# A hybrid attention, state-space and convolution layer: 24 modulation tiles moved from two projection loops into the attention heads

## Chip, cores and metric

One Trainium2 chip, one core. The metric is the time of one execution on the device in microseconds (us), lower is better. In the rows PE is TensorE (matmuls), PEld its weight loads, DVE is VectorE, ACT is ScalarE, POOL is GpSimd and SP is the engine that only starts transfers. Each engine runs its instructions in the order in which they stand in its queue; an instruction that waits holds up everything behind it on that engine.

## What is computed

One layer of a diffusion backbone in float32, for 128 context tokens (with the vector `c_ctx`) and 512 latent tokens (with the vector `c`). Cut to what matters:

```python
mod = silu(c_vec) @ w_ada + b_ada                  # 6 x 1024 numbers for each vector
sh1, sc1, g1, sh2, sc2, g2 = split(mod, 6)
h = rmsnorm(x) * (1 + sc1) + sh1
cq, ckv, kr, z, xs, Bm, Cm, dt, gm, gs = split(h @ w_in)
q = rmsnorm(cq) @ w_uq; k, v = mla_kv(rmsnorm(ckv), kr, w_ukv)   # 8 heads, rotary on latents
p = softmax(q @ k.T * scale); o_mla = (p @ v) @ w_o_mla
xbc = silu(dwconv(xs, Bm, Cm)); y = chunked scan, both directions
o_ssd = rmsnorm(y * silu(z)) @ w_o_ssd
merged = sigmoid(gm) * o_mla + sigmoid(gs) * o_ssd
x = x + g1 * (merged @ w_out)
h2 = rmsnorm(x) * (1 + sc2) + sh2
u = dwconv(h2 @ w_up); x = x + g2 * ((silu(u1) * u2) @ w_down)
```

The change concerns the rows of `mod` that make `g1`, `sh2` and `sc2`: three times 1024 numbers, which is 24 tiles of 128 numbers, each for two vectors. They are first read in the output projection `w_out` (`g1`) and after it (`sh2`, `sc2`).

## The kernel before

All 640 tokens lie along the free axis and the features on the 128 partitions. A large product is made of three matmuls on rounded halves of both operands (`mm3`, L139): high by high, low by high, high by low. Each weight tile is loaded raw (`wload`, L129, the pool `ws` with four buffers of the tag `raw`), rounded by ACT (L115, `whi`) and its remainder made by POOL, or for some small tiles by DVE (L112, `wlo`). The order of PE is written out by hand.

**A modulation tile.** 16 modulation tiles are made on PE at the start. The other 32 are row products on DVE (`ada_rows`, L242 to L263): tile j has one load of 512 KB, a 128x1024 block of `w_ada` turned so that the outputs lie on the partitions (`araw`); two SCALAR_TENSOR_TENSOR of 128x1024 multiply it with the two conditioning vectors, laid on all partitions (`crow`, after a SiLU), and sum along the row into two columns of `mod` (L260); one TENSOR_SCALAR adds the bias to both columns (L261). Tiles 16 to 23 are gate 1, 24 to 31 shift 2, 32 to 39 scale 2 and 40 to 47 gate 2. Each call of `ada_next` makes one tile, with its instructions put behind that of the eviction given to it. The first eight stand in the loop over the eight row blocks of `w_o_mla` (after L837), eight in the loop over `w_o_ssd` (after L1093) and eight in the loop over `w_out` (after L1103); gate 2 is made later and is not touched.

**A head of the attention.** Eight heads run one behind the other, some 32.6 us each. The scores part has four blocks of 128 latent queries against 640 keys and one block of 128 context queries (`pc`). A block t puts its scores into two PSUM tiles of 128x320 (tag `sm`, four banks in a ring), then DVE takes the two row maxima (L591, TENSOR_REDUCE) and scales them (L592), ACT takes the exponentials out of both PSUM tiles (L594), DVE adds the two row sums (L598), inverts (L599) and normalises the block `p` (L600). So a bank is free for a later product when the exponential has read it, and the exponential waits for L592. With the ring of four, block 2 takes the banks of block 0, block 3 those of block 1, `pc` the first of block 2; then the query product of the next head, `lowrank` (L139 with `cqh`), takes the second bank of block 2 and the first of block 3. In an odd head the rotary queries of the next pair of heads come ahead of it (`rope_queries`): their weight is 256 wide and its remainder `wlo` is made by DVE. After the scores the values part turns the probabilities around (`flip`, L607, with the rounding on ACT and the remainder `ptl` on DVE, L112) and multiplies them with the values (L616). Between these products `fill` puts matmuls of other projections (`w_xbc`, `w_gm`), whose convolution (L465, L468, two instructions of 127 and two of 511 columns) or eviction runs on DVE and ACT. F_S, F_P, F_R, F_Q, F_K, F_T and F_V say how many fill products stand where; they do not change.

**The loops after.** In the `w_o_ssd` loop DVE evicts the PSUM tile `big` of each row block (L1092), adds the attention's share (L1093), and makes the remainder for `w_out` (L112); the next row block but one needs the bank that L1092 reads.

Of the kernel before, what the change touches and what calls it, by code (L numbers as in the profile page):

```python
# [10 lines left out]
F32 = mybir.dt.float32  # L11
# [46 lines left out]
D1, D2 = 2, 4  # L58
G0, G_T, G_C, G_S, G_Z, G_B, G_Y = 15, 1, 1, 1, (2, 2, 3, 2, 4), 3, 0
RP = 2  # L60


CHUNKS = (0, 8, 16)
# [16 lines left out]
def trunk_kernel(ctx: ExitStack, tc: tile.TileContext, a: dict):  # L80
# [15 lines left out]
    def page(dt=F32, pool=None):  # L96
        return (pool or pg).tile([128, T], dt, tag="pgr", name=nm("pg"))
# [141 lines left out]
        DVE.tensor_reduce(st[:m, 0:n, :], pt[:m].rearrange("p (i g r) -> p i r g", g=4, r=32)[:, :, 0:2, :], AX.X, ALU.add)  # L239
        return st  # L240

    def ada_rows(tiles, tile, nraw):  # L242


        crow = []
        for r in range(2):
            t = tile("crow", 2)
            nc.sync.dma_start(t, a["crow"][r : r + 1, :].to_broadcast([128, D]))
            ACT.activation(t, t, AF.Silu)
            crow.append(t)  # L250
        left = list(tiles)

        def step(after):
            j = left.pop(0)
            raw = tile("araw", nraw)
            nc.sync.dma_start(raw, a["w_adar"][j - 16])
            with tc.issue_after(after.ins):
                for r in range(2):
                    out = raw if r else tile("junk", 1)
                    DVE.scalar_tensor_tensor(out, raw, 1.0, crow[r], ALU.mult, ALU.mult, accum_out=mod[:, j, r : r + 1])  # L260
                DVE.tensor_scalar(mod[:, j, :], mod[:, j, :], vec[:, V_BADA + j : V_BADA + j + 1], None, ALU.add)  # L261

        return step  # L263
# [230 lines left out]
    def fill(n):  # L494
        for _ in range(n):
            next(streams[0], None)
# [1 line left out]

    att = ExitStack()
    ost = ExitStack()  # L500
    op = ost.enter_context(tc.tile_pool(name="op", bufs=8, side="right", reuse_waits="tile"))
    awk = ExitStack()
    ap = awk.enter_context(tc.tile_pool(name="ap", bufs=1, reuse_waits="tile"))

    cos = ap.tile([128, NS], F32)
    nc.scalar.dma_start(cos, a["rope"][0])
# [67 lines left out]
    def scores(q, qr, k, c0, ks, p):  # L574

        n = ks.stop - ks.start
        qc = slice(c0, c0 + 128)
        w = min(n, 320)
        parts = []
        for n0 in range(0, n, w):  # L580
            ps = small()
            parts.append((ps[:, 0:w], slice(ks.start + n0, ks.start + n0 + w)))
        mm3(parts, q[0][:, qc], q[1][:, qc], k, True, False)

        for k_ in krs:
            for sv, sl in parts:
                PE.matmul(sv, qr[:, qc], k_[:, sl], start=False, stop=k_ is krs[1])  # L587
        st = ap.tile([128, 8], F32, tag="st", name=nm("st"), bufs=6)
        n = len(parts)
        for i, (sv, _) in enumerate(parts):  # L590
            DVE.reduce_max(st[:, i : i + 1], sv, AX.X)  # L591
        DVE.tensor_scalar(st[:, 2:3], st[:, 0:1], st[:, n - 1 : n], -SCALE, ALU.max, ALU.mult)  # L592
        for i, (sv, _) in enumerate(parts):
            ACT.activation(  # L594
                p[:, i * w : (i + 1) * w], sv, AF.Exp, bias=st[:, 2:3], scale=SCALE, accum_out=st[:, 4 + i : 5 + i]
            )
        if n == 2:
            DVE.tensor_tensor(st[:, 4:5], st[:, 4:5], st[:, 5:6], ALU.add)  # L598
        DVE.reciprocal(st[:, 3:4], st[:, 4:5])  # L599
        DVE.tensor_scalar(p, p, st[:, 3:4], None, ALU.mult)  # L600

    def flip(probs, kt):

# [70 lines left out]
    with tc.manual_schedule(engines={PE.engine}):  # L674
# [8 lines left out]
        for h in range(H):  # L683
            hh = h % 2
            probs = []
            for t in range(4):
                p = ap.tile([128, 640], F32, tag="p", name=nm("p"), bufs=4)
                scores(q, qrs[hh], k, NP + 128 * t, keys, p)
                probs.append(p)
                fill(F_S[t])  # L690
            pc = ap.tile([128, 128], F32, tag="pc", name=nm("pc"))
            scores(q, qrs[hh], k, 0, ctx_keys, pc)
# [8 lines left out]
                q = next(qk)  # L701
                fill(F_Q)
            fill(F_K if nxt else F_K + 2)
            o = page(F32, op)
            oT.append(o)
            pts = []
            for kt in range(LAG):
# [5 lines left out]
            for kt in range(5):  # L713
# [4 lines left out]
                if kt + LAG < 5:  # L718
                    pts.append(flip(probs, kt + LAG))
                elif kt + LAG == 5:  # L720
                    ptc = flip([pc], 0)
                fill(F_V[kt])
            ACT.copy(o[:, NP:T], po)
            po = small()
# [92 lines left out]
    next(dec)  # L817

    mg = []
    ar = att.enter_context(tc.tile_pool(name="ar", bufs=1, reuse_waits="tile"))  # L820
    ada_next = ada_rows(range(16, 24), lambda tag, bufs: ar.tile([128, D], F32, tag=tag, name=nm(tag), bufs=bufs), NR1)
    with tc.manual_schedule(engines={PE.engine}):
        for m in range(8):
            if m == D1:
# [13 lines left out]
            d = tc.dram_tile([128, T], F32, name=f"scr_mg{m}")  # L838
            nc.sync.dma_start(d, t)
            mg.append(d)  # L840
            ada_next(ev)
    att.close()


# [227 lines left out]
    mp = mst.enter_context(tc.tile_pool(name="mp", bufs=16, side="right", reuse_waits="tile"))  # L1072
    mer = []
    sxs = ExitStack()
    sx = sxs.enter_context(tc.tile_pool(name="sx", bufs=1, side="right", reuse_waits="tile"))
    ada_next = ada_rows(range(24, 40), lambda tag, bufs: sx.tile([128, D], F32, tag=tag, name=nm(tag), bufs=bufs), 2)
    with tc.manual_schedule(engines={PE.engine}):
        for m in range(8):
            whi, wlo = ahead.pop(0) if ahead else wload(a["w_o_ssd"][m], 1024)
# [14 lines left out]
            hi, lo = page(F32R, mp), page(F32R, mp)  # L1094
            split(hi, lo, t)
            mer.append((hi, lo))
            ada_next(ev)

    def residual(dst, ps, gcol, src, cols):
        for r, g in GROUPS:  # L1100
# [28 lines left out]
    for m in range(8):  # L1129
# [12 lines left out]
        if 0 < m < 7:  # L1142
            cc = PARTS[0] if keep else slice(0, T)
            POOL.tensor_tensor(acc[:, cc], acc[:, cc], sq[:, cc], ALU.add)
        ada_next(ev)
        scale_col(a2[:, m, :], mod[:, 32 + m, :], V_GFFN + m)
        x1.append(x)
        x1d.append(tc.dram_tile([128, T], F32, name=f"scr_x{m}"))
# [607 lines left out]
```

## Time and profile before

| | us |
|---|---|
| median of three runs | 1274.91 |
| lowest and highest run | 1271.58 and 1274.96 |
| the profiled execution, whole time | 1274.9 |
| its span from first to last instruction | 1273.1 |
| PE busy in the span | 1205.2 (95%) |
| DVE busy | 877.2 (69%) |
| ACT busy, POOL busy | 588.3 (46%), 531.0 (42%) |

The page of the profile gives for each engine its busy time and its share of the span. A view by windows gives the same for each stretch, with the clock that TensorE was granted as a share of its full 2.4 GHz (PEclk). A timeline gives each instruction with its start, its duration, and in square brackets how long its engine stood idle before it and whose result ended that. The attention runs from 119 to 380 us, the `w_o_mla` loop from 400 to 456, the `w_o_ssd` loop from 660 to 723, the `w_out` loop to 780.

### The profile page before, as it was taken

The page shows a single profiled execution, that of the slowest core. Times are in us where ns is not written, and L with a number is a line of the kernel's source. Part 1 is how long each engine was busy: PE and PEld are TensorE (multiplying, and loading weights), DVE is VectorE, ACT ScalarE, POOL GpSimd, SP SyncE. Part 2 cuts the span into 40 slices and gives each one's busy share as a digit, 9 for nine tenths or more (in the row PEclk, how much of TensorE's full clock was granted, in tenths as well). Part 3 has the DMA queues.
Part 4 walks back from the last instruction along what each step waited for, and adds up shares of the span by engine and source line. Part 5 has one row for each costly group of instructions (what it writes and reads, how often), then busy time and mean ns, then how long its engine had stood idle before and what let it go on. Part 6 is the DMA issues. An engine that isn't in the chain of part 4 may idle for free. (4 is left out here: it accounts for less than half of the span.)

```text
span 1273.1 us, 21205 instructions
## 1 busy us (share of the span) xinstructions
PE 1205.2 (95%) x8289; PEld 1152.4 (91%) x8289; DVE 877.2 (69%) x1520; ACT 588.3 (46%) x1083; POOL 531.0 (42%) x336
## 2 busy tenths in 40 slices
PE   7798999999999899899988998999899999999996
PEld 5698999989999897788888898999899999999996
DVE  4766656565547668666869999777885555875755
ACT  5455455544647644444862233543333433434432
POOL 3433121211213349754767383534355333454422
PEclk9899999999999899899989899999999999999998
DMA  8333221222128551213374674233246221352212
GB/s 331 113 107 114 70 76 57 77 71 98 48 96 297 198 183 67 96 66 100 117 257 172 212 247 165 83 120 104 87 145 232 72 79 39 108 200 74 87 71 83
DMA packets 58821, 159.80 MB, mean 126 GB/s; under 512 B 6752, under 2 KB 12704, under 8 KB 58720
## 3 DMA queue, kind: packets, MB, share of 16 engines
q1 hardware_dynamic: 56960, 156.33, 36.2%
q10 hardware_dynamic: 1760, 2.11, 0.6%
q8 instruction: 65, 1.06, 0.4%
q14 instruction: 36, 0.29, 0.1%
HBM read 130.30 MB, written 25.59 MB: 122 GB/s over the span
## 5 line engine op out<-in xcount | busy, mean ns | idle before, releaser
L139 PE MATMUL big<-pg,whi 128*128 128x384 f32 (+2 forms) x3264 | 639.0, 315 | 13.7 <-DVE pg L468 8.3
L139 PEld LDWEIGHTS big<-pg,whi 128*128 128x128 f32 x3264 | 501.5, 191 | 28.0 <-issue 15.5
L112 POOL TENSOR_TENSOR wlo<-raw,whi 128x512 fp32r<-128x512 f32 (+3 forms) x161 | 304.8, 1900 | 509.7 <-ACT whi L115 496.7
L139 PE MATMUL big<-pg,wlo 128*128 128x384 f32 (+2 forms) x1632 | 385.8, 312 | 4.3 <-POOL wlo L112 4.2
L139 PEld LDWEIGHTS big<-pg,wlo 128*128 128x128 f32 x1632 | 257.3, 191 | 5.7 <-POOL wlo L112 5.2
L115 ACT CAST whi<-raw 128x512 fp32r<-128x512 f32 (+3 forms) x186 | 138.2, 758 | 148.8 <-issue 67.3
L139 PE MATMUL sm<-pg,whi 128*128 128x320 f32 (+2 forms) x584 | 135.8, 318 | 5.9 <-ACT pg L115 2.4
L139 PEld LDWEIGHTS sm<-pg,whi 128*128 128x128 f32 x584 | 100.6, 192 | 9.3 <-ACT pg L115 2.8
L139 PE MATMUL sm<-pg,wlo 128*128 128x320 f32 (+2 forms) x292 | 92.0, 315 | 0.4 <-POOL wlo L112 0.4
L465 DVE SCALAR_TENSOR_TENSOR st<-big,vec,st 128x127 f32<-128x127 f32 x68 | 37.0, 544 | 65.5 <-ACT st L463 65.5
L112 POOL TENSOR_TENSOR wlo<-sum,whi 128x512 fp32r<-128x512 f32 (+1 forms) x40 | 51.2, 1300 | 60.1 <-ACT whi L115 60.1
L115 ACT CAST pg<-pg 128x640 fp32r<-128x640 f32 (+1 forms) x60 | 40.4, 706 | 69.9 <-DVE pg L1093 35.5
L112 DVE TENSOR_TENSOR pg<-pg,pg 128x640 fp32r<-128x640 f32 (+1 forms) x57 | 54.1, 972 | 11.8 <-ACT pg L115 11.8
L260 DVE SCALAR_TENSOR_TENSOR araw<-araw,crow 128x1024 f32<-128x1024 f32 x32 | 60.0, 1874 | 0.6
L139 PEld LDWEIGHTS sm<-pg,wlo 128*128 128x128 f32 x292 | 56.0, 192 | 0.7 <-POOL wlo L112 0.7
L112 DVE TENSOR_TENSOR ptl<-sm,pth 128x512 fp32r<-128x512 f32 (+1 forms) x48 | 29.6, 620 | 35.1 <-ACT pth L610 35.1
L594 ACT ACTIVATE p<-sm,st 128x320 f32<-128x320 f32 x64 | 33.1, 523 | 37.6 <-DVE st L592 37.6
L591 DVE TENSOR_REDUCE st<-sm 128x1 f32<-128x320 f32 (+1 forms) x72 | 31.6, 463 | 26.5 <-PE sm L587 26.5
L260 DVE SCALAR_TENSOR_TENSOR junk<-araw,crow 128x1024 f32<-128x1024 f32 x32 | 45.8, 1431 | 0.0
L610 ACT CAST pth<-sm 128x512 fp32r<-128x512 f32 (+1 forms) x48 | 25.5, 533 | 43.7 <-PE sm L607 43.7
L465 DVE SCALAR_TENSOR_TENSOR pg<-big,vec,pg 128x127 f32<-128x127 f32 (+1 forms) x42 | 22.8, 543 | 31.2 <-ACT pg L463 31.2
L115 ACT CAST whi<-sum 128x512 fp32r<-128x512 f32 (+1 forms) x40 | 22.6, 596 | 38.9 <-DVE sum L1335 30.0
(325 smaller groups left out, 2000.2 us busy)
## 6 DMA issues: line engine op xcount, KB each, us to landing
raw<-w_up SPq DMA_DIRECT2D x44, 512.0 KB, 3.4
araw<-w_adar SPq DMA_DIRECT2D x32, 512.0 KB, 4.2
araw<-w_ada SPq DMA_DIRECT2D x16, 512.0 KB, 7.6
raw<-w_down SPq DMA_DIRECT2D x16, 512.0 KB, 3.6
raw<-w_xbc SPq DMA_DIRECT2D x12, 512.0 KB, 3.4
scr_xc<-pg SPq DMA_DIRECT2D x16, 320.0 KB, 3.4
pg<-scr_xc SPq DMA_DIRECT2D x16, 320.0 KB, 4.5
raw<-w_gm SPq DMA_DIRECT2D x8, 512.0 KB, 3.2
```

Of the source, the lines that this page charges most:

```text
L112: return eng.tensor_tensor(out, x, f(hi), ALU.subtract)
L115: ACT.copy(hi, src)
L139: PE.matmul(o, w, r[:, s], start=first and i == 0, stop=last and i == 2, skip_group_check=on)
L260: DVE.scalar_tensor_tensor(out, raw, 1.0, crow[r], ALU.mult, ALU.mult, accum_out=mod[:, j, r : r + 1])
L465: DVE.scalar_tensor_tensor(dst[:, lo_ + 1 : hi_], p[:, lo_ : hi_ - 1], vec[:, w : w + 1], dst[:, lo_ + 1 : hi_], ALU.mult, ALU.add)
L591: DVE.reduce_max(st[:, i : i + 1], sv, AX.X)
L594: ACT.activation(p[:, i * w : (i + 1) * w], sv, AF.Exp, bias=st[:, 2:3], scale=SCALE, accum_out=st[:, 4 + i : 5 + i])
L610: return ph, pl, ACT.copy(ph[:, :n], pt[:, :n]), sub(DVE, pl[:, :n], pt[:, :n], ph[:, :n])
```

## The change

The 24 tiles of gate 1, shift 2 and scale 2 leave the three loops and stand in the attention, beside heads 0 to 5 (`LA = 6`), four tiles to a head in eight half steps. The first half step of a tile handles the vector of index 0 in two SCALAR_TENSOR_TENSOR of 128x512 (into `junk`, which now shares the buffer of the rotation's `sw`), followed by a TENSOR_SCALAR that adds the bias and the second partial sum. The second half step handles index 1 in one 128x1024 instruction, written over the raw tile, and a TENSOR_SCALAR for the bias. Four half steps stand behind the normalise of the four score blocks, four in the values loop behind the remainders `ptl`. The raw tiles come from the `ws` ring of four that the weight loads use; the two `crow` tiles are loaded ahead of the attention and lie in the pool `op`, whose page buffers fall from 8 to 6: heads 6 and 7 put their outputs in the `crow` buffers. Two of the three earlier pairs of `crow` loads with their SiLU go.

```diff
+LA = 6
+    def halves_of(left, crow, tile, ap):
+        now = []
+        def step(after):
+            if not now:
+                if not left:
+                    return
+                j = left.pop(0)
+                raw = tile("raw", RAW)
+                nc.sync.dma_start(raw, a["w_adar"][j - 16])
+                now.extend([(j, raw, 0), (j, raw, 1)])
+            j, raw, r = now.pop(0)
+            with tc.issue_after(after.ins):
+                col, bias = mod[:, j, r : r + 1], vec[:, V_BADA + j : V_BADA + j + 1]
+                if r:
+                    DVE.scalar_tensor_tensor(raw, raw, 1.0, crow[r], ALU.mult, ALU.mult, accum_out=col)
+                    DVE.tensor_scalar(col, col, bias, None, ALU.add)
+                else:
+                    junk, two = tile("junk", 1), ap.tile([128, 1], F32, tag="two", name=nm("two"), bufs=2)
+                    for c, o in ((slice(0, NS), col), (slice(NS, D), two)):
+                        DVE.scalar_tensor_tensor(junk, raw[:, c], 1.0, crow[r][:, c], ALU.mult, ALU.mult, accum_out=o)
+                    DVE.tensor_scalar(col, col, bias, two, ALU.add, ALU.add)
+        return step
...
-    op = ost.enter_context(tc.tile_pool(name="op", bufs=8, side="right", reuse_waits="tile"))
+    op = ost.enter_context(tc.tile_pool(name="op", bufs=LA, side="right", reuse_waits="tile"))
+    def ada_tile(tag, bufs):
+        if tag == "junk":
+            return ap.tile([128, NS], F32, tag="sw", name=nm(tag))
+        return (op if tag == "crow" else ws).tile([128, D], F32, tag=tag, name=nm(tag), bufs=bufs)
+    ada_half = ada_rows(range(16, 40), ada_tile, 0, ap)
...
-                scores(q, qrs[hh], k, NP + 128 * t, keys, p)
+                ev = scores(q, qrs[hh], k, NP + 128 * t, keys, p)
                 probs.append(p)
+                if h < LA:
+                    ada_half(ev)
                 fill(F_S[t])
...
+                if h < LA and kt < 4:
+                    ada_half(pts[-1][3])
                 fill(F_V[kt])
...
-    ada_next = ada_rows(range(16, 24), lambda tag, bufs: ar.tile([128, D], F32, tag=tag, name=nm(tag), bufs=bufs), NR1)
-            ada_next(ev)
-    ada_next = ada_rows(range(24, 40), lambda tag, bufs: sx.tile([128, D], F32, tag=tag, name=nm(tag), bufs=bufs), 2)
-            ada_next(ev)
-        ada_next(ev)
```

What this does to the order of instructions on an engine shows at three places. A row gives the line, the operation, what it writes and reads, and its shape; the lines of the changed kernel are some 37 higher in the attention (L628, L629, L637 for L591, L592, L600; L495 and L498 for L465 and L468).

DVE in the scores part of head 2, before: from the normalise of block 0 (`p_2088`) to the scaled maximum of block 3 (`st_2187`).

```order
L600 TENSOR_SCALAR p_2088<-p_2088,st_2101 128x640
L591 TENSOR_REDUCE st_2151<-sm_2139 128x1
L598 TENSOR_TENSOR st_2123<-st_2123 128x1
L591 TENSOR_REDUCE st_2151<-sm_2140 128x1
L599 RECIPROCAL st_2123<-st_2123 128x1
L592 TENSOR_SCALAR st_2151<-st_2151 128x1
L600 TENSOR_SCALAR p_2110<-p_2110,st_2123 128x640
L591 TENSOR_REDUCE st_2187<-sm_2175 128x1
L591 TENSOR_REDUCE st_2187<-sm_2176 128x1
L598 TENSOR_TENSOR st_2151<-st_2151 128x1
L592 TENSOR_SCALAR st_2187<-st_2187 128x1
```

The same engine and head after: block 0's `p_2166` and block 1's `p_2195` are normalised, and then come the scaled maxima of block 2 (`st_2238`) and block 3 (`st_2281`).

```order
L637 TENSOR_SCALAR p_2166<-p_2166,st_2179 128x640
L265 SCALAR_TENSOR_TENSOR junk_2190,mod<-raw_2188,crow_776 128x512
...
L265 SCALAR_TENSOR_TENSOR junk_2190,two_2191<-raw_2188,crow_776 128x512
...
L637 TENSOR_SCALAR p_2195<-p_2195,st_2208 128x640
L260 SCALAR_TENSOR_TENSOR raw_2188,mod<-raw_2188,crow_779 128x1024
L629 TENSOR_SCALAR st_2238<-st_2238 128x1
...
L637 TENSOR_SCALAR p_2225<-p_2225,st_2238 128x640
L265 SCALAR_TENSOR_TENSOR junk_2249,mod<-raw_2247,crow_776 128x512
L498 SCALAR_TENSOR_TENSOR st_2260<-big_1967,vec,st_2260 128x511
L265 SCALAR_TENSOR_TENSOR junk_2249,two_2250<-raw_2247,crow_776 128x512
L629 TENSOR_SCALAR st_2281<-st_2281 128x1
```

Two half steps now stand ahead of the scaled maximum of block 2, and a third one, the normalise of block 2 and the four convolution instructions ahead of that of block 3.

DVE in head 3, before: the remainder `wlo_2578` of the rotary query weight stands behind the normalise of block 2 (`p_2479`).

```order
L592 TENSOR_SCALAR st_2492<-st_2492 128x1
L600 TENSOR_SCALAR p_2451<-p_2451,st_2464 128x640
...
L592 TENSOR_SCALAR st_2520<-st_2520 128x1
L600 TENSOR_SCALAR p_2479<-p_2479,st_2492 128x640
L112 TENSOR_TENSOR wlo_2578<-raw_2575,whi_2577 128x256
L465 SCALAR_TENSOR_TENSOR st_2535<-big_2323,vec,st_2535 128x127
```

The same place after, where the remainder is `wlo_2710` and the normalised blocks 2 and 3 are `p_2602` and `p_2637`.

```order
L637 TENSOR_SCALAR p_2602<-p_2602,st_2615 128x640
L265 SCALAR_TENSOR_TENSOR junk_2626,mod<-raw_2624,crow_776 128x512
...
L498 SCALAR_TENSOR_TENSOR st_2667<-big_2419,vec,st_2667 128x511
L265 SCALAR_TENSOR_TENSOR junk_2626,two_2627<-raw_2624,crow_776 128x512
...
L637 TENSOR_SCALAR p_2637<-p_2637,st_2650 128x640
L260 SCALAR_TENSOR_TENSOR raw_2624,mod<-raw_2624,crow_779 128x1024
L636 RECIPROCAL st_2695<-st_2695 128x1
L114 TENSOR_TENSOR wlo_2710<-raw_2707,whi_2709 128x256
```

The remainder has moved behind the normalise of block 3 and behind all four half steps of the scores.

DVE in the `w_o_ssd` loop, before: one row block of the loop.

```order
L1092 TENSOR_TENSOR pg_7394<-big_7345,pg_7394 128x640
L1093 TENSOR_TENSOR pg_7398<-pg_7398,pg_7394 128x640
L260 SCALAR_TENSOR_TENSOR junk_7408,mod<-araw_7406,crow_7097 128x1024
L112 TENSOR_TENSOR pg_7403<-pg_7398,pg_7402 128x640
L260 SCALAR_TENSOR_TENSOR araw_7406,mod<-araw_7406,crow_7100 128x1024
L261 TENSOR_SCALAR mod<-mod,vec 128x2
```

The same engine and loop after: two row blocks.

```order
L1128 TENSOR_TENSOR pg_7531<-big_7482,pg_7531 128x640
L1129 TENSOR_TENSOR pg_7535<-pg_7535,pg_7531 128x640
L114 TENSOR_TENSOR pg_7540<-pg_7535,pg_7539 128x640
L1128 TENSOR_TENSOR pg_7598<-big_7549,pg_7598 128x640
L1129 TENSOR_TENSOR pg_7602<-pg_7602,pg_7598 128x640
```

The three instructions of the modulation tile are gone from between the eviction's own.

## Rows read from the trace of the kernel before

**Rows 1.** The page, busy time of each engine and its share of the span.
```profile
PE 1205.2 (95%) x8289; PEld 1152.4 (91%) x8289; DVE 877.2 (69%) x1520; ACT 588.3 (46%) x1083; POOL 531.0 (42%) x336
```

**Rows 2.** Windows: length; busy us (instructions) of each engine; PEclk, DMA share, GB/s.
```profile
146.00:380.00 234.00, 230.52 (x1554) 222.43 (x1553) 136.01 (x327) 119.57 (x277) 46.88 (x23) 1.00 0.21 71
660.00:700.00 40.00, 35.37 (x221) 34.55 (x220) 35.12 (x32) 14.23 (x19) 28.30 (x12) 0.94 0.59 212
```

**Rows 3.** What PE waited for, 380 to 900: total us, times, longest.
```profile
PE big L139 <- DVE pg L1092: 4.5, 2, 3.1
...
PE big L139 <- POOL wlo L112: 2.7, 1, 2.7
...
PE sm L166 <- POOL pg L1144: 1.8, 1, 1.8
```

**Rows 4.** Timeline of the `w_o_ssd` loop and its end, DVE and PE.
```profile
667.71 2.60 DVE L260 SCALAR_TENSOR_TENSOR junk<-araw,crow 128x1024 f32<-128x1024 f32 x1
...
673.17 2.58 DVE L260 SCALAR_TENSOR_TENSOR araw<-araw,crow 128x1024 f32<-128x1024 f32 x1
...
675.68 0.81 DVE L1092 TENSOR_TENSOR pg<-big,pg 128x640 f32<-128x640 f32 x1
...
676.64 0.82 PE L139 MATMUL big<-pg,whi 128*128 128x384 f32 x4 [1.47 <-DVE pg L1092]
...
720.95 0.81 DVE L1092 TENSOR_TENSOR pg<-big,pg 128x640 f32<-128x640 f32 x1
...
723.43 0.69 PE L139 MATMUL sm<-pg,whi 128*128 128x384 f32 x1 [2.43 <-ACT pg L115]
```

**Rows 5.** Windows of equal length in that loop, at half and at full clock.
```profile
695.70:699.10 3.40, 3.40 (x15) 3.40 (x15) 3.36 (x6) 1.11 (x2) 2.21 (x1) 0.50 0.95 334
699.10:702.50 3.40, 3.40 (x25) 3.40 (x25) 3.37 (x4) 0.50 (x1) 1.26 (x1) 1.00 0.94 284
```

**Rows 6.** Instructions of L260 and L261: duration in ns, min/median/max.
```profile
L260 DVE SCALAR_TENSOR_TENSOR junk<-araw,crow x32: 1208/1218/2914, 402.3 to 902.8; 128x1024 f32<-128x1024 f32 x32
...
L260 DVE SCALAR_TENSOR_TENSOR araw<-araw,crow x32: 1195/1226/3311, 403.7 to 905.1; 128x1024 f32<-128x1024 f32 x32
...
L261 DVE TENSOR_SCALAR mod<-mod,vec x32: 215/230/2244, 405.1 to 906.5; 128x2 f32<-128x2 f32 x32
```

**Rows 7.** DVE's groups by shape, 146 to 380: busy us, mean ns.
```profile
L600 DVE TENSOR_SCALAR p<-p,st 128x640 f32<-128x640 f32 x28 | 15.4, 549 | 0.4
...
L465 DVE SCALAR_TENSOR_TENSOR st<-big,vec,st 128x511 f32<-128x511 f32 x8 | 5.9, 740 | 0.0
```

**Rows 8.** Timeline of head 2, end of its scores part: DVE, POOL, ACT and PE.
```profile
193.98 0.21 DVE L592 TENSOR_SCALAR st<-st 128x1 f32<-128x1 f32 x1
...
194.94 2.40 POOL L112 TENSOR_TENSOR wlo<-raw,whi 128x1024 fp32r<-128x1024 f32 x1 [6.99 <-ACT whi L115]
...
196.13 1.22 DVE L598 TENSOR_TENSOR st<-st 128x1 f32<-128x1 f32 x1
...
197.28 0.20 DVE L592 TENSOR_SCALAR st<-st 128x1 f32<-128x1 f32 x1
...
197.51 0.53 ACT L594 ACTIVATE p<-sm,st 128x320 f32<-128x320 f32 x1 [0.90 <-DVE st L592]
...
198.48 0.46 PE L139 MATMUL sm<-cqh,pg 128*128 128x320 f32 x2
```

**Rows 9.** Windows of the scores parts of head 2 and head 3.
```profile
186.40:202.90 16.50, 15.53 (x108) 15.27 (x107) 13.76 (x37) 8.49 (x25) 3.95 (x2) 1.00 0.20 69
220.00:236.00 16.00, 16.00 (x113) 16.00 (x112) 9.72 (x32) 8.56 (x26) 2.40 (x1) 1.00 0.18 60
```

**Rows 10.** Timeline of head 3: DVE's first scaled maximum and `wlo`, PE's wait for it.
```profile
219.75 0.21 DVE L592 TENSOR_SCALAR st<-st 128x1 f32<-128x1 f32 x1
...
226.58 0.42 DVE L112 TENSOR_TENSOR wlo<-raw,whi 128x256 fp32r<-128x256 f32 x1
...
228.73 0.46 PE L139 MATMUL sm<-cqh,wlo 128*128 128x320 f32 x2
```

More of the change, by code (lines that the diff above doesn't have):

```diff
@@ L240, in col_sums, with ada_rows @@
         return st
-    def ada_rows(tiles, tile, nraw):
+    def halves_of(left, crow, tile, ap):
[20 more added lines that the diff above has]
+        return step
+    def ada_rows(tiles, tile, nraw, half=None):
         crow = []
@@ L251, in ada_rows @@
         left = list(tiles)
+        if half is not None:
+            return halves_of(left, crow, tile, half)
         def step(after):
@@ L599, in scores @@
         DVE.reciprocal(st[:, 3:4], st[:, 4:5])
-        DVE.tensor_scalar(p, p, st[:, 3:4], None, ALU.mult)
+        return DVE.tensor_scalar(p, p, st[:, 3:4], None, ALU.mult)
     def flip(probs, kt):
@@ L703, in trunk_kernel @@
             fill(F_K if nxt else F_K + 2)
-            o = page(F32, op)
+            o = page(F32, op) if h < LA else op.tile([128, D], F32, tag="crow", name=nm("o"), bufs=2)[:, 0:T]
             oT.append(o)
@@ L819, in trunk_kernel @@
     mg = []
-    ar = att.enter_context(tc.tile_pool(name="ar", bufs=1, reuse_waits="tile"))
-    ada_next = ada_rows(range(16, 24), lambda tag, bufs: ar.tile([128, D], F32, tag=tag, name=nm(tag), bufs=bufs), NR1)
     with tc.manual_schedule(engines={PE.engine}):
@@ L1074, in trunk_kernel @@
     sxs = ExitStack()
-    sx = sxs.enter_context(tc.tile_pool(name="sx", bufs=1, side="right", reuse_waits="tile"))
-    ada_next = ada_rows(range(24, 40), lambda tag, bufs: sx.tile([128, D], F32, tag=tag, name=nm(tag), bufs=bufs), 2)
     with tc.manual_schedule(engines={PE.engine}):
```

## Prediction, made before the changed kernel was run

> **What bounds the kernel now.** Read the page first: PE is busy 95% of the span and DVE 69% [rows 1], so the time is PE's work plus what PE waits for. The windows come next. In 146 to 380, the attention without its first part, PE is busy 230.5 of 234 us at full clock, and DVE 136.0; in 660 to 700, the `w_o_ssd` loop, PE is busy 35.4 of 40 and DVE 35.1 [rows 2]. So a DVE saving can pay where the tiles leave and has little to give where they arrive. PE's waits say how much the first is: 4.5 us for the eviction L1092, 2.7 for a remainder of POOL, 1.8 for L1144 [rows 3]. The timeline shows the mechanism of the first: the eviction at 675.68 begins when the second row product of a modulation tile ends, and PE resumes at 676.64 after 1.47 us of waiting [rows 4]. The other such wait is the 3.1 that is the longest [rows 3].
>
> **What is removed.** The 4.5 us for L1092 go. Behind the longer wait PE's clock is at half for 3.40 us and does 15 matmuls there, against 25 in the next 3.40 [rows 5]: 10/25 x 3.40 = 1.4 us go with it. The wait of 2.43 us at 723.43 stays: its eviction starts at 720.95, directly when the products are done, and the chain behind it has no modulation tile in it [rows 4]. Of the 1.8 for L1144, in the `w_out` loop, I take half, 0.9, with the ends 0 and 1.8. In the `w_o_mla` loop I take 1.0 of 2.7 for POOL's remainder, between 0 and 2.7: an undisturbed remainder takes 2.40 [rows 8], and the wait would be shorter, not gone. Sum: 4.5 + 1.4 + 0.9 + 1.0 = **7.8 us gained**. With the upper ends and a half-clock stretch of 1.4 behind each of those two waits it is 4.5 + 1.4 + 1.8 + 2.7 + 2.8 = 13.2; with the lower ends 5.9. The two `crow` pairs that go free ACT and SP, which no wait of PE in these rows names: nothing.
>
> **What a half step costs DVE.** A 128x1024 row product takes 1.22 us at the median, the bias 0.23 [rows 6]. No row has a 128x512 one. Half of 1.22 is 0.61, and the convolution's 128x511 instruction takes 0.74 [rows 7]; I take 0.7, nearer the row. First half step: 0.7 + 0.7 + 0.23 = 1.63. Second: 1.22, about 0.08 more to the next start, and 0.2: 1.5. A head takes four of each: 4 x 3.13 = 12.5 us, of which 6.3 stand in the scores part, and 24 tiles take 75.
>
> **Even heads.** DVE is busy 13.76 of 16.5 us in the scores part of head 2 [rows 9]. With 6.3 more it is 20.0, so that part is longer by at least 3.5 unless work leaves it, and by the order none does. Step by step: the scaled maximum of block 2 stands at 193.98 [rows 8]. Two half steps now come ahead of it, 3.1 us; DVE's idle time there hides almost none of it, because the block's maxima arrive while DVE is busy anyway: 197.05. From there to the scaled maximum of block 3 the order has a bias (0.2), two maxima (1.0), the small ones (0.5), the normalise of block 2 (0.55), the four convolution instructions (2.2) and two half-width products (1.4): 5.8, so it ends near 202.9 and not 197.5 [rows 8]. The exponential that frees the bank runs 0.23 behind it for 0.53 (197.51) and ends at 198.04; PE's query product starts at 198.48 [rows 8], so 0.44 was spare. The move is 5.4, less that 0.44, less 0.2 of DVE's idle: **4.75 us of stall**, in part already at `pc`. Nothing can fill it: PE's order is fixed. Three such heads: 14.3. The ends are 3.5, by the sum, and 5.4.
>
> **Odd heads.** In head 3 DVE has room in sum (9.72 of 16 [rows 9], 16.0 with the half steps), but not in order. From the first scaled maximum, 219.75, to the end of `wlo`, 227.00, there are 7.25 us; PE wants `wlo` at 228.73 [rows 10]. By the order after, four half steps (6.3), one more normalise (0.55), four convolution instructions (2.2) and the small ones of block 3 and `pc` (0.9) come between; some 1.2 of DVE's waits there are filled. 7.25 + 9.95 - 1.2 = 16.0, so `wlo` ends at 235.75: **7.0 us of stall**. In the values part a 1.22 us product now stands ahead of a remainder `ptl`; I take 2.0 a head, between 0 and 4 x 1.22. Head 3: 9.0. In head 1 `wlo` stands ahead of the last half step (less 0.55 and 1.22, so 5.2 + 2.0 = 7.2); in head 5 there is no convolution on DVE either, but one other remainder (3.7 + 2.0 = 5.7). Odd heads: 21.9. Together **36.2 us lost**, between 10.5 (the sum for the even heads, nothing for the odd) and 47 (3 x 5.4, and 4.9 in each odd head's values part).
>
> **Clock.** Six stalls of 3.5 us and more stand beside a wait of 3.1 us that was followed by 3.40 us at half clock, worth 1.4 [rows 3, 5]. I take 1.4 each, **8.4**, between 0 and twice that.
>
> **What is taken at nothing.** 24 loads of 512 KB move on SP's queue into a stretch whose DMA share is 0.21 [rows 2]. They take turns with the weights in a ring of four, so a weight's load now waits for a second half step, and the rounding of that weight stands in ACT's queue ahead of exponentials. The ring's lead hides this by my walk; if not, one more half step is lost in a head, 6 x 1.5 = 9. POOL's own queue is unchanged.
>
> **Sum.** 1274.9 (profiled run, 1273.1 span, equal to the median 1274.91) - 7.8 + 36.2 + 8.4 = 1311.7, so **1312 us**.
>
> **A page against this change.** At 196.13 a DVE instruction on 128x1 takes 1.22 us and ends with POOL's remainder of 194.94 + 2.40 [rows 8], and beside POOL a row product takes 2.60 and not 1.22 [rows 4, 6]. The Trainium skill, "GPSIMD Engine Reference", section 8 "Key points", says that GpSimd shares its SBUF interfaces with VectorE, in contention with VectorE's instructions that have two SBUF inputs. By that rule, which these rows bear out, the row products do not fit beside POOL's remainders at their undisturbed price. Its price is the third rival's.
>
> **Rivals.** *First, the attention absorbs the tiles (faster).* The place is DVE's 98 idle us in 146 to 380 [rows 2]; if half steps ran whenever DVE has nothing due and the banks were still free in time, only the gain would show: 1274.9 - 7.8 = **1267**, to 1262 with the upper end. It decides if the scaled maxima of blocks 2 and 3 move by less than the 0.44 us that the query product has to spare. For it: 98 us against 75. Against it: the order puts the half steps ahead of these maxima. 0.15. *Second, gain and loss cancel.* Only the sum for even heads is lost, 3 x 3.5 = 10.5, without clock: 1274.9 + 10.5 - 7.8 = **1278**, 1269 to 1290 with half of the odd heads' loss. 0.15. *Third, POOL and the clock make it worse.* Each head has two remainders of POOL; a product that meets one lasts 2.60 - 1.22 = 1.38 longer. 12 meetings on the path are 16.6, and twice the clock price is 8.4 more: 1312 + 8 to 25, **1328**. 0.15. Of the clock the Trainium skill, "TensorE: Matmul & The Clock Gate", section "HAM oscillation — how this bites in real kernels", shows a kernel that turned cold at every step of a loop because of a wait in each; the half clock behind one wait here agrees [rows 5], and whether it would come in each head no row here shows.
>
> **How the numbers follow.** The forecast (1290 to 1320) has 0.55, the rivals 0.15 each. A measurement of this kernel tells about 0.3%, 3.8 us, from no change: below 1271 is faster, above 1279 slower. Faster: the first rival and a little of the second, 0.17. Same: part of the second, 0.07. Slower: 0.76. The range leaves out the lower part of the first rival and the upper of the third: 1266 to 1334.
>
> **What would show it.** Right: in the windows of heads 0 to 5 each head is 4 to 9 us longer and heads 6 and 7 are not; PE waits there for exponentials in even heads and for DVE's `wlo` in odd ones; DVE is near 90% busy in 146 to 380; the waits for L1092 are gone; half-clock stretches appear in the attention. Wrong: heads of 32 to 34 us, or the loss in only one kind of head, or a weight that PE waits for, which would be the ring.

## The result and the profile after

The changed kernel takes 1286.72 us (median of 4 runs, 1284.08 to 1288.24) beside 1274.68 for the kernel before: ratio 1.0099, 95% interval 1.0075 to 1.0122. It is slower by 12 us. The forecast was 1312: the direction is right, the change is forecast three times too large. The profiled span is 1284.4 us.

The page after, where [rows 1] stood: PE has 6 us more of busy time (it runs longer at half clock) and DVE 39 less.

```profile
PE 1211.2 (94%) x8289; PEld 1155.0 (90%) x8289; DVE 838.3 (65%) x1592; ACT 582.2 (45%) x1078; POOL 518.3 (40%) x336
```

What PE waited for in heads 0 to 5 after (total us, times, longest). L141, L114, L624, L631 and L653 are the L139, L112, L587, L594 and L616 of before.

```profile
PE sm L141 <- ACT p L631: 11.8, 9, 3.1
PE sm L141 <- DVE wlo L114: 5.4, 2, 4.1
PE sm L624 <- POOL qr L114: 1.8, 2, 1.0
PE sm L653 <- DVE ptl L114: 1.7, 3, 0.6
```

No wait for the load of a weight is among them, so the ring of four, which the forecast took at nothing, cost nothing that PE's waits show.

The windows of heads 0 to 5 after, where [rows 2] had the attention as a whole (length; busy us of PE, PEld, DVE, ACT, POOL; granted clock, DMA share, GB/s). Heads 1, 2 and 3 are the long ones and the only ones below full clock. DVE is busy for 184.9 of these 233.3 us, 79%, where the forecast had near 90%.

```profile
120.40:156.70 36.30, 34.17 (x229) 33.07 (x228) 29.66 (x84) 15.12 (x38) 6.04 (x2) 1.00 0.24 82
156.70:196.50 39.80, 35.99 (x228) 34.25 (x226) 29.59 (x81) 18.20 (x40) 6.24 (x4) 0.91 0.37 123
196.50:239.10 42.60, 37.51 (x220) 35.31 (x219) 33.88 (x85) 16.37 (x39) 7.60 (x5) 0.88 0.29 95
239.10:281.70 42.60, 37.30 (x236) 35.38 (x235) 30.95 (x83) 19.93 (x45) 7.60 (x4) 0.92 0.34 115
281.70:316.70 35.00, 32.40 (x211) 30.54 (x211) 32.33 (x86) 15.73 (x37) 6.12 (x4) 1.00 0.33 111
316.70:353.70 37.00, 34.79 (x232) 32.79 (x232) 28.49 (x82) 20.26 (x45) 9.52 (x4) 1.00 0.50 161
```

PE runs the same products in nearly the same order in both kernels, so the start of one product in both traces tells how far the kernel has slipped there. By that the time went and came as follows (us, changed minus before; waits are PE's idle stretches over 0.1):

| stretch of before | change | PE's waits, before and after | time at half clock, before and after |
|---|---|---|---|
| up to head 0 (119) | +1.3 | 17.3, 16.1 | 10.2, 17.1 |
| head 0 | +2.3 | 0, 2.1 | 0, 0 |
| head 1 | +6.4 | 0.5, 3.8 | 0, 6.8 |
| head 2 | +8.9 | 1.0, 5.1 | 0, 10.2 |
| head 3 | +8.6 | 0, 5.3 | 0, 6.8 |
| head 4 | +0.9 | 2.1, 2.6 | 0, 0 |
| head 5 | +3.1 | 0, 2.2 | 0, 0 |
| heads 6, 7 | +0.4 | 0, 0.1 | 0, 0 |
| `w_o_mla` loop (380 to 458) | -6.0 | 5.2, 1.7 | 6.8, 0 |
| 458 to 540 | -3.0 | 4.7, 4.7 | 10.2, 3.4 |
| 540 to 662 | -0.5 | 4.8, 3.9 | 6.8, 6.7 |
| `w_o_ssd` loop (to 723) | -8.2 | 4.6, 0 | 3.8, 0.1 |
| `w_out` loop (to 780) | -4.5 | 5.1, 1.5 | 9.8, 3.4 |
| the rest | +1.5 | 14.3, 16.1 | 14.2, 15.9 |

The attention loses 30.7 us: 17.7 in waits, and 13.0 more that stand mostly in heads 1 to 3, beside 23.9 us of half clock. The stretch from 380 to 780 gives 22.2.

Two rows differ from run to run, and no run ties them to the change. The stretch up to head 0 is between 1.7 us shorter and 1.0 longer in the profiles of the three runs below whose edit stands behind it (one loop without its tiles). The stretch from 458 to 540 is 3.5 us shorter in the run without the `w_o_ssd` tiles, whose edit begins behind it, and 0.2 shorter in two versions of the changed kernel (`wlo` on POOL, and POOL's remainders left out).

**Inside head 2.** DVE, ACT, POOL and PE at the place of [rows 8] (timeline: start, duration, engine; L629 is the scaled maximum, L260 the second half step).

```profile
205.67 2.54 POOL L114 TENSOR_TENSOR wlo<-raw,whi 128x1024 fp32r<-128x1024 f32 x1 [5.02 <-ACT whi L117]
...
205.88 3.42 DVE L260 SCALAR_TENSOR_TENSOR raw<-raw,crow 128x1024 f32<-128x1024 f32 x1
...
209.22 0.20 DVE L629 TENSOR_SCALAR st<-st 128x1 f32<-128x1 f32 x1
...
214.16 0.21 DVE L629 TENSOR_SCALAR st<-st 128x1 f32<-128x1 f32 x1
...
214.40 0.53 ACT L631 ACTIVATE p<-sm,st 128x320 f32<-128x320 f32 x1 [3.81 <-DVE st L629]
...
215.07 0.64 PE L141 MATMUL sm<-cqh,pg 128*128 128x320 f32 x1 [1.78 <-ACT p L631]
```

The chain of the forecast is there link by link: half step, scaled maximum of block 3, exponential, query product. From the first scaled maximum shown to the second there are 4.94 us (5.8 forecast). The second half step takes 3.42 us here beside POOL's remainder, and not 1.22; what that is worth follows below. Head 3 after, where [rows 10] stood:

```profile
252.45 0.41 DVE L114 TENSOR_TENSOR wlo<-raw,whi 128x256 fp32r<-128x256 f32 x1
...
252.91 0.90 PE L141 MATMUL sm<-cqh,wlo 128*128 128x320 f32 x2 [4.09 <-DVE wlo L114]
```

PE waits 4.09 us for `wlo`; the forecast had 7.0.

### The profile page after: what moved, and what is told of

The parts are those of the page before. It is cut to its first block, busy times and chain, and to the rows that moved or that the text cites. A ratio compares the mean times of both kernels' runs of the same rounds, so it can differ in the third digit from the quotient of the medians.

```text
span 1284.4 us, 21256 instructions
## 1 busy us (share of the span) xinstructions
PE 1211.2 (94%) x8289; PEld 1155.0 (90%) x8289; DVE 838.3 (65%) x1592; ACT 582.2 (45%) x1078; POOL 518.3 (40%) x336
## 5 line engine op out<-in xcount | busy, mean ns | idle before, releaser
L141 PE MATMUL big<-pg,whi 128*128 128x384 f32 (+2 forms) x3264 | 637.0, 314 | 11.0 <-DVE pg L498 9.3
L141 PEld LDWEIGHTS big<-pg,whi 128*128 128x128 f32 x3264 | 500.2, 190 | 24.6 <-issue 10.0
L114 POOL TENSOR_TENSOR wlo<-raw,whi 128x512 fp32r<-128x512 f32 (+3 forms) x161 | 291.4, 1818 | 518.5 <-ACT whi L117 496.8
L141 PE MATMUL big<-pg,wlo 128*128 128x384 f32 (+2 forms) x1632 | 383.8, 311 | 1.6 <-POOL wlo L114 1.6
L141 PEld LDWEIGHTS big<-pg,wlo 128*128 128x128 f32 x1632 | 255.9, 190 | 2.3 <-POOL wlo L114 2.0
L141 PE MATMUL sm<-pg,whi 128*128 128x320 f32 (+2 forms) x584 | 135.4, 316 | 5.6 <-DVE o L1400 1.9
L141 PEld LDWEIGHTS sm<-pg,whi 128*128 128x128 f32 x584 | 99.8, 190 | 9.9 <-DVE o L1400 2.7
L141 PE MATMUL sm<-pg,wlo 128*128 128x320 f32 (+2 forms) x292 | 91.5, 313 | 0.0
L495 DVE SCALAR_TENSOR_TENSOR st<-big,vec,st 128x127 f32<-128x127 f32 x68 | 37.0, 543 | 64.7 <-ACT st L493 64.7
L114 POOL TENSOR_TENSOR wlo<-sum,whi 128x512 fp32r<-128x512 f32 (+1 forms) x40 | 50.7, 1289 | 61.4 <-ACT whi L117 61.4
L114 DVE TENSOR_TENSOR pg<-pg,pg 128x640 fp32r<-128x640 f32 (+1 forms) x55 | 50.4, 938 | 19.7 <-ACT pg L117 19.7
L141 PEld LDWEIGHTS sm<-pg,wlo 128*128 128x128 f32 x292 | 55.6, 190 | 0.0
L631 ACT ACTIVATE p<-sm,st 128x320 f32<-128x320 f32 x64 | 33.2, 525 | 42.1 <-DVE st L629 42.1
L114 DVE TENSOR_TENSOR ptl<-sm,pth 128x512 fp32r<-128x512 f32 (+1 forms) x48 | 29.8, 622 | 27.1 <-ACT pth L647 26.9
L495 DVE SCALAR_TENSOR_TENSOR pg<-big,vec,pg 128x127 f32<-128x127 f32 (+1 forms) x42 | 22.8, 543 | 29.2 <-ACT pg L493 29.2
L628 DVE TENSOR_REDUCE st<-sm 128x1 f32<-128x320 f32 (+1 forms) x72 | 31.3, 460 | 12.7 <-PE sm L624 12.7
L498 DVE SCALAR_TENSOR_TENSOR st<-big,vec,st 128x127 f32<-128x127 f32 x68 | 37.2, 547 | 1.7
L1297 ACT ACTIVATE pg<-pg 128x640 f32<-128x640 f32 x22 | 16.3, 739 | 48.2 <-DVE pg L498 48.2
```

The costliest lines, as they stand in the source:

```text
L114: return eng.tensor_tensor(out, x, f(hi), ALU.subtract)
L141: PE.matmul(o, w, r[:, s], start=first and i == 0, stop=last and i == 2, skip_group_check=on)
L495: DVE.scalar_tensor_tensor(dst[:, lo_ + 1 : hi_], p[:, lo_ : hi_ - 1], vec[:, w : w + 1], dst[:, lo_ + 1 : hi_], ALU.mult, ALU.add)
L498: DVE.scalar_tensor_tensor(dst[:, lo_ : hi_ - 1], p[:, lo_ + 1 : hi_], vec[:, w + 2 : w + 3], dst[:, lo_ : hi_ - 1], ALU.mult, ALU.add)
L631: ACT.activation(p[:, i * w : (i + 1) * w], sv, AF.Exp, bias=st[:, 2:3], scale=SCALE, accum_out=st[:, 4 + i : 5 + i])
L1297: ACT.activation(u, u, AF.Silu)
```

## Experiments

Theory after the result: the half steps cost time only where they stand ahead of a block's scaled maximum or of `wlo` (order, not sum), the half clock roughly doubles the price where such waits are long, and the three loops gave back far more than the forecast's 7.8 us. The rival: the loss is DVE's sum of work, and the loops' gain in the trace is partly chance of the clock.

### Neither place: the 24 tiles left out

```diff
-    ada_half = ada_rows(range(16, 40), ada_tile, 0, ap)
+    for r in range(2):
+        DVE.tensor_scalar(mod[:, 16:40, r], vec[:, V_BADA + 16 : V_BADA + 40], 0.0, None, ALU.add)
...
-                    ada_half(ev)
...
-                    ada_half(pts[-1][3])
```

> The changed kernel without the row products of the 24 tiles and without their loads and the crow rows: their columns of mod hold the bias alone, so the outputs are not the reference's. Theory A (aligned traces: the tiles cost 22 us in the loops they left and about 31 in the attention, plus 1.3 ahead of it): about 1253 us, with no waits for exponentials or wlo in the attention and full clock there. Theory B (the forecast's gain of 7.8 was right and the rest of the 22 us is chance of the clock): about 1267.

Measured: 1252.70, ratio to the kernel before 0.9836 (0.9802 to 0.987). So by the medians the tiles cost 21.6 us where they stood before (by the interval 17 to 25) and 34.0 where they stand after, and the difference is the result. Between the traces of the two kernels the attention differs by 30.7. In the trace of this version each head is as long as before, within 0.03 us; the `w_o_mla` loop is 5.2 shorter, the `w_o_ssd` loop 8.3, the `w_out` loop 6.0, and 780 to 1000 is 5.7 longer, of which more below. That is 13.8 in all; 3.5 more are the stretch at 458 to 540, and for the rest of the 21.6 the trace shows no place.

### Only the scores parts, only the values parts

```diff
-    ada_half = ada_rows(range(16, 40), ada_tile, 0, ap)
...
+    ada_half = ada_rows([j for j in range(16, 40) if j % 4 < 2], ada_tile, 0, ap)
...
-                if h < LA and kt < 4:
-                    ada_half(pts[-1][3])
```

> The changed kernel with only the half steps of the scores parts (two tiles a head, 12 in all); the 12 tiles of the values parts hold the bias alone. Theory A (the loss comes from half steps ahead of the scaled maxima, which hold PSUM banks): nearly the whole loss stays, 1253 + 26 = about 1279. Theory B (the loss is DVE's sum of work, wherever in a head it stands): half of it, about 1268.

The other has `j % 4 > 1` and leaves out the call behind `scores`.

> The changed kernel with only the half steps of the values parts (12 tiles); the 12 tiles of the scores parts hold the bias alone. Theory A: 1253 + 4 = about 1257, waits only for ptl (0.6 a time). Theory B: about 1268.

Measured: 1276.19 (ratio 1.0013, 0.9993 to 1.0033) with the scores' half steps, 1258.66 (0.988, 0.9855 to 0.9905) with the values'. Twelve tiles each, the same amount of work, cost 23.5 us in one part of a head and 6.0 in the other. The rival's 1268 for both is out. PE's waits in heads 0 to 5, first of the scores version and then of the values version (its L633 and L655 are the exponential and the values product):

```profile
PE sm L141 <- ACT p L633: 11.2, 7, 3.1
PE sm L141 <- DVE wlo L114: 4.5, 2, 4.1
```

```profile
PE sm L655 <- DVE ptl L114: 2.8, 4, 1.3
PE sm L646 <- DVE kl L114: 1.1, 1, 1.1
PE sm L141 <- ACT p L633: 0.4, 1, 0.4
```

The 23.5 + 6.0 are 4.5 short of the 34.0 that both together cost, which is no more than the noise of these medians; in the traces the attention loses 23.2, 4.9 and 30.7.

The two halves alone leave one rival: that DVE is short of time within the scores part, which is fuller than the values part. Heads 3 and 4 speak against it. In head 3 the 6.3 us of half steps of a scores part still fit ([rows 9]: 9.72 and 6.3 in 16.0), yet PE waits 4.8 us for `wlo` and an exponential. In head 4 they do not fit, by 3.3 us, yet PE waits 1.4 for exponentials. Head 4's scores part before (DVE busy 12.97):

```profile
254.00:270.00 16.00, 15.01 (x104) 14.75 (x103) 12.97 (x34) 7.34 (x22) 3.88 (x2) 1.00 0.15 51
```

### `wlo` on POOL

```diff
-        uh, ul = wload(a["w_rv"][hp][:, 0:256], 256, DVE)
+        uh, ul = wload(a["w_rv"][hp][:, 0:256], 256)
```

> The changed kernel, with the remainder wlo of the rotary query weight (128x256) made by POOL and not by DVE. Theory A (in odd heads the order of DVE, not its sum, makes PE wait): the waits of 4.1 and 1.3 us for wlo in heads 3 and 5 go, the exponential of pc is next about 2 us earlier than PE now resumes, and less half clock follows in head 3: 1286.7 - 4 to 8, about 1281. Theory B (DVE is late anyway): the same time appears as a wait for the next exponential, about 1286.

Measured: 1285.75 (1.0075, 1.0046 to 1.0104). That is where the second theory had it, but the interval reaches down to the first theory's 1281 too. The trace shows what happened. The 4.1 us for `wlo` are gone, but PE then stops a few products later, for the remainder of the next weight, which also stands behind the half steps in DVE's queue: 3.31 us. Head 3 is 1.4 us shorter than in the changed kernel, head 4 as long. In head 5 the wait of 1.3 for `wlo` goes without such a return, and the head is 1.6 shorter.

```profile
PE sm L141 <- ACT p L631: 11.7, 9, 3.1
PE sm L141 <- DVE pg L114: 3.3, 1, 3.3
```

Order is not all of that wait. The remainder takes 2.75 us beside a remainder of POOL; in the changed kernel, where POOL is idle there, the same instruction takes 0.68.

```profile
251.05 3.74 POOL L114 TENSOR_TENSOR wlo<-raw,whi 128x1024 fp32r<-128x1024 f32 x1 [4.95 <-ACT whi L117]
...
252.59 2.75 DVE L114 TENSOR_TENSOR pg<-raw,pg 128x512 fp32r<-128x512 f32 x1
```

### More products ahead of the wait

```diff
-F_S, F_P, F_R, F_Q, F_K = (0, 1, 1, 2), 1, 1, 1, 2
+F_S, F_P, F_R, F_Q, F_K = (0, 1, 1, 2), 3, 1, 1, 0
```

> The changed kernel with two of the fill products (each six matmuls, some 0.9 us) moved from behind the next head's queries (F_K 2 to 0) to ahead of them (F_P 1 to 3), so that PE has 1.8 us more to do before it wants the banks of blocks 2 and 3. Theory A (the exponentials are late by a fixed amount in each head): waits of 3.1, 1.8, 4.1, 0.9 and 1.3 us shrink by up to 1.8 each, some 7, with 3 to 6 of clock: about 1275. Theory B (DVE is short of time in sum): the wait comes back at the flips, 1284 to 1288.

Measured: 1275.14 (1.0005, 0.9983 to 1.0027), as the first theory said; the move gives back nearly all that the change lost. Between the two traces the attention is 11.6 us shorter. In head 1 the waits fall from 3.8 to 2.1 and 6.8 us of half clock disappear: 4.1 us for 1.7 us of waiting. In head 2 the waits fall by 1.8, the half clock from 10.2 to 3.4 us, and the head is 4.1 shorter too. PE's waits for exponentials fall from 11.8 to 7.3. Of the windows of heads 1 and 2 in this version, the first is at full clock and the second nearly (0.91 and 0.88 in the changed kernel).

```profile
PE sm L141 <- ACT p L631: 7.3, 7, 2.1
...
PE sm L141 <- DVE wlo L114: 2.3, 1, 2.3
```

```profile
156.00:191.50 35.50, 33.39 (x226) 31.67 (x225) 29.71 (x81) 18.34 (x40) 6.12 (x4) 1.00 0.42 136
191.50:230.20 38.70, 35.41 (x221) 33.39 (x220) 32.28 (x85) 16.39 (x39) 8.82 (x5) 0.96 0.31 107
```

### POOL's remainders out of the attention

```diff
+            if name in ("xbc", "gm"):
+                raw = ws.tile([128, 1024], F32, tag="raw", name=nm("raw"), bufs=RAW)
+                nc.sync.dma_start(raw, a["w_" + name][m])
+                hi, lo = wpair()
+                ACT.copy(hi, raw)
+                ACT.copy(lo, raw)
...
```

> The changed kernel where the remainder of the w_xbc and w_gm weights in the attention is a second rounded copy on ACT and no instruction of POOL, so these products are not the reference's. Theory A (a row product beside POOL's remainder is held until that ends: 3.42 us against 1.22 in head 2, and that is on the path): head 2's first wait of 2.2 goes, with a part of its half clock: 2 to 5 us faster, 1282 to 1285. Theory B (the hold is hidden): same time, or slower by what ACT's extra copy (1.05 us each) delays exponentials, 1287 to 1290.

Measured: 1289.66 (1.0115, 1.0072 to 1.0158). As a time it settles nothing: the edit also reaches the stage ahead of the attention, which is 5.0 us longer. The trace answers a part of the question. The half step of head 2 that took 3.42 beside POOL takes 1.22, and the wait of 2.21 behind it is gone, but the next one grows from 1.78 to 3.10. By these two waits 0.9 us of the hold was on the path; the edit also gives ACT a second copy for each of these weights, ahead of exponentials, and the trace does not part the two.

```profile
209.18 1.22 DVE L260 SCALAR_TENSOR_TENSOR raw<-raw,crow 128x1024 f32<-128x1024 f32 x1
```

```profile
216.18 0.64 PE L141 MATMUL sm<-cqh,pg 128*128 128x320 f32 x1 [3.10 <-ACT p L638]
```

### What each loop gave: one loop without its eight tiles

Each is the kernel before without `ada_next(ev)` in one loop, with the bias alone in its eight columns.

```diff
-            ada_next(ev)
```

> The kernel before, without the eight tiles of the w_o_mla loop (gate 1 holds the bias alone, so outputs are not the reference's). Theory A (that loop's two PE waits and the half clock behind them, and the shorter half clock of the stage at 500 to 540, come from its tiles): 1274 - 5.2 - 3.2, about 1266. Theory B (as forecast: only 1.0 us of POOL's remainder): 1273. If the stage at 500 to 540 is unchanged: 1269.

> The kernel before, without the eight tiles of the w_o_ssd loop (shift 2 holds the bias alone). Theory A: both waits for the eviction and the half clock behind the longer one go, and nothing else: 1274 - 8, about 1266. Theory B (forecast: 4.5 + 1.4): about 1268. Theory C (the saved time is waited for again in the w_out loop): 1271 or more.

> The kernel before, without the eight tiles of the w_out loop (scale 2 holds the bias alone). Theory A (the waits at 723 and 774 and the half clock behind each depend on these tiles): 1274 - 6, then 2 to 4 back at 780 to 1000: about 1271. Theory B (forecast: 0.9): about 1273.

Measured: 1264.99 (0.9939, 0.9915 to 0.9962), 1261.55 (0.99, 0.9862 to 0.9938) and 1272.88 (0.9984, 0.9962 to 1.0006). The three gains, 9.1, 12.6 and 1.2 us, come to 22.9, beside 21.6 with all left out; their intervals reach 3, 5 and 3 us to each side. The third is not clear of none. The traces show less of each: 5.3 in the `w_o_mla` loop, 8.0 from the `w_o_ssd` loop to 1000, and a loss of 2.0 from the `w_out` loop to 1000. The stretch at 458 to 540 is 1.6, 3.5 and 0.4 us shorter in them; the second of these cannot come of tiles that stand behind it.

*`w_o_mla`.* The trace gives 5.3 us in the loop, with waits of 5.2 down to 1.2 and no half clock. The tiles were in ACT's way and not only in DVE's: before, ACT alternates between two functions and loads a table nine times for thirteen activations; without the tiles its order is another and it loads three of the nine less. ACT's groups of table loads in the loop, of the kernel before and of this one (the sigmoid is L830; the other function L856 and L855; busy us, mean ns):

```profile
L830 ACT ACT_TABLE_LOAD x5 | 6.4, 1283 | 0.1
...
L856 ACT ACT_TABLE_LOAD x4 | 5.1, 1283 | 0.1
```

```profile
L855 ACT ACT_TABLE_LOAD x3 | 3.8, 1283 | 0.2 <-issue 0.2
L830 ACT ACT_TABLE_LOAD x3 | 3.8, 1283 | 0.1
```

What this does to PE shows at one small tile, `eh`, that ACT rounds for a product of PE. Before, it stands behind a table load and a sigmoid:

```profile
420.46 1.28 ACT L830 ACT_TABLE_LOAD   x1
...
422.39 0.53 ACT L115 CAST eh<-ac 128x160 fp32r<-128x160 f32 x2
...
423.35 0.66 PE L806 MATMUL sm<-cons,eh 128*128 128x128 f32 x4 [2.32 <-DVE eh L112]
```

Without the tiles it stands ahead of both, and PE does not wait there:

```profile
415.00 0.55 ACT L115 CAST eh<-ac 128x160 fp32r<-128x160 f32 x2
...
415.56 1.28 ACT L830 ACT_TABLE_LOAD   x1
```

*`w_o_ssd`.* 8.3 us in the loop: 1.6 and 3.2 for the two waits, 1.35 for the half clock, 0.6 in between, and 1.3 of the wait at 723, which falls from 2.43 to 1.10. The trace of before shows why that wait hangs on the tiles: PE's last product for the bank is over by 717.3, and DVE begins the eviction only at 720.95, when the bias of a modulation tile ends (2.23 us beside a remainder of POOL, 0.23 at the median).

```profile
718.80 2.23 DVE L261 TENSOR_SCALAR mod<-mod,vec 128x2 f32<-128x2 f32 x1
```

*`w_out`.* 3.4 us less in the loop and 5.4 more from 780 to 1000. Most of that is the clock: 10.2 us at half clock there, none before, and 1.5 more of waits. The kernel before and this one have the same wait for L468 (3.64 and 3.63 us); behind it the clock stays full in the one and is half in the other. Windows behind that wait, of the kernel before and then of this one:

```profile
895.50:899.00 3.50, 3.50 (x24) 3.50 (x25) 3.50 (x8) 1.14 (x2) 1.59 (x1) 1.00 0.00 0
```

```profile
892.90:896.00 3.10, 3.10 (x12) 3.10 (x13) 3.10 (x7) 1.14 (x2) 1.58 (x1) 0.50 0.00 0
896.00:899.00 3.00, 3.00 (x15) 3.00 (x14) 2.88 (x5) 0.00 (x0) 0.00 (x0) 0.60 0.60 175
```

### A placement that beats both kernels

Gate 1 and shift 2 in the values parts of heads 0 to 5 and the scores parts of heads 4 and 5, scale 2 back in the `w_out` loop.

```diff
-    ada_half = ada_rows(range(16, 40), ada_tile, 0, ap)
+    ada_half = ada_rows(range(16, 32), ada_tile, 0, ap)
...
-                if h < LA:
+                if h in (4, 5):
                     ada_half(ev)
...
+    ada_next = ada_rows(range(32, 40), lambda tag, bufs: sx.tile([128, D], F32, tag=tag, name=nm(tag), bufs=bufs), 2)
...
+        ada_next(ev)
         scale_col(a2[:, m, :], mod[:, 32 + m, :], V_GFFN + m)
```

> All 24 tiles are made: gate 1 and shift 2 in the values parts of heads 0 to 5 and the scores parts of heads 4 and 5 alone, scale 2 in the w_out loop as in the kernel before. Theory A (costly are only the scores parts of heads 0 to 3): 1253, plus 4 for the values parts, 3 for heads 4 and 5, 4 for the w_out loop: about 1264, faster than both kernels. Theory B (DVE's sum): 1253 + 16/24 x 31 + 4 = about 1278.

Measured: 1267.04, ratio to the kernel before 0.9952 (0.9931 to 0.9973). Its heads 0 to 4 lose 2.7 us in all, and head 5 loses 5.7, of which 3.3 are a wait for `wlo`. With `wlo` on POOL as well:

> All 24 tiles made, as in the version with the scores parts of heads 4 and 5 only and scale 2 in the w_out loop (1267.0), and wlo of the rotary query weight on POOL. Theory A: the 3.3 us wait for wlo in head 5 goes, nothing else moves: about 1263.5. Theory B (POOL's queue is now ahead of the remainders that fill products need): same or slower, 1267 to 1270.

Measured: 1265.37, ratio 0.9929 (0.9901 to 0.9956). The two medians are too near each other to tell this version from the last. In the trace head 5 is 3.5 us shorter, so there the wait for `wlo` goes, as the first theory had it, and does not come back. One more product ahead of the wait (`F_P` 2, `F_K` 1):

> All 24 tiles made, as in the version with the scores parts of heads 4 and 5 only, scale 2 in the w_out loop and wlo on POOL (1265.4), with one fill product moved from behind the next head's queries to ahead of them (F_P 2, F_K 1). Theory A (1.4 us of waits for exponentials are left there): 1 to 2 us faster, 1264. Theory B (the remainders ptl wait longer instead): same or slower, 1265 to 1268.

Measured: 1265.59 (0.9927, 0.9901 to 0.9952), no difference from the version without it, as the second theory had it. The trace shows the exchange in head 1: the wait of 0.66 us for an exponential goes, and the wait for `ptl` grows from 0.71 to 1.15.

## Why the prediction was wrong

Between the forecast's 1312 and the measured 1286.7 lie 25 us. By the medians 13.8 of them are in the gain (7.8 forecast, 21.6 measured) and 10.6 in the loss (36.2 and 8.4 for the clock, so 44.6 forecast, 34.0 measured). Both terms were mis-sized, to the same side, and neither is the larger beyond noise.

**What bounds the kernel, and the mechanism of the loss: right but for head 1.** DVE's saving in the attention has no worth, the half steps delay scaled maxima and `wlo`, PE waits for exponentials in even heads and for `wlo` in heads 3 and 5. In head 1 the forecast had 5.2 us for `wlo`; PE waits there for an exponential, 3.09, and not for `wlo`. That the place in a head decides and not DVE's sum of work is shown by the two halves (23.5 against 6.0 us).

**The gain, 7.8 us: sized far too small.** It is 21.6 with the tiles left out, of which the trace places 13.8, a little above the forecast's upper end of 13.2.

- *The `w_o_ssd` loop* was sized at 5.9 and is 8.3. Most of the difference is the wait at 723, which I kept whole because I read that its eviction starts when the products are done. That reading was wrong: the bias of a modulation tile stands ahead of that eviction and ends as it starts, and without the tiles the wait halves.
- *The `w_o_mla` loop* was sized at 1.0, as a shorter remainder of POOL; it is 5.3 in the loop, because ACT's order changes and both waits with the half clock behind them go. This is the largest step that failed in the gain: the wait of 2.3 for `eh` in that loop was in no term of the sum, and POOL's remainder, which comes late because ACT does, was only taken to be shorter.
- *The stage from 458 to 540* was not in the sum and gave 3.0, with waits unchanged and 6.8 us less of half clock. It differs as much between runs whose edit stands behind it, so it is not shown to come of the tiles.
- *The `w_out` loop* (0.9 forecast, 1.2 measured and not clear of none) was right by luck: the trace has 3.4 gained in the loop and 5.4 lost behind it.

I priced each wait by what one row of it said and gave nothing to what stands around it.

**Heads 0, 4 and 5: failed by extrapolation.** Head by head the forecast, with its 1.4 for the clock, was 6.2, 8.6, 6.2, 10.4, 6.2 and 7.1. Measured in the trace: 2.3, 6.4, 8.9, 8.6, 0.9 and 3.1. Heads 0, 4 and 5 come to 6.3 against 19.4. I had walked head 2 with its convolution on DVE between the half steps and taken heads 0 and 4 for alike. In head 4 no convolution stands ahead of the scaled maximum of block 3, and its waits for exponentials are 0.5 and 0.9. In head 0 it stands ahead of that of block 2, and one wait of 2.1 comes of it. The 2.0 us for `ptl` in the values part of each odd head were 0.6.

**The stalls of heads 1 to 3, and the clock.** Heads 1 to 3 come to 23.9 against 25.2, and that is luck: each stall was sized too high and the clock too low. New waits are 3.4, 4.1 and 5.3 us against 7.2, 4.75 and 9.0, and 11.1 us stand beyond the waits, in the heads with half clock, against 4.2. It may be that the half clock takes up time that I had counted as waiting, since DVE catches up while PE is slower; no run separates that. The half steps themselves were sized right: the half-width product takes 0.68 (0.7), its bias 0.27, the full one 1.22.

**The third rival's POOL.** The row product of 3.42 us beside POOL's remainder, against a median of 1.22, ended 1.1 us after the remainder did (209.30 and 208.21), about its own time later. So it was held, as the small instruction of [rows 8] was. Its price on the path was about 0.9 us in head 2, and nothing like the 16.6 over all shows. The rule cited there from the Trainium skill ("GPSIMD Engine Reference", section 8 "Key points") agrees with these rows; as a price it decided little.

**The first rival, absorption,** holds for the values parts almost (6.0 us for twelve tiles) and for the scores parts of head 4.

**What stays open:** why the same wait is followed by half clock in one run and not in another. This is so behind L468, in head 1 (waits of 3.3 and 3.1 us, 6.8 and 0 us of half clock, in the changed kernel and in the one without POOL's remainders) and in head 0 (a wait of 2.1 us, 0 and 3.4 us of half clock, in the changed kernel and in the one with `wlo` on POOL). Some 4 to 8 us of the 21.6 have no place in the traces.

## What to carry to other kernels

Work that fills an engine's idle time is nearly free only behind the instructions that somebody waits for: ask of each insertion point which PSUM bank or weight is released by what stands next in that queue, and put the work behind it. A forecast of a saving needs the same care as one of a cost: leave the work out altogether as the first experiment, since that splits any move into what it gains and what it pays. Walk each kind of repetition once (here: heads by where the convolution stands) before multiplying.

## What the runs showed that was not expected

Taking DVE instructions out of a loop changed ACT's order there and saved three of nine table loads of 1.28 us. And 1.7 us less of waiting in a head gave 4.1 us, because the half clock behind it went too.
